# Two attentions of a transformer block's first stage in one sequence of 32 rounds, with other dense products between

## The chip, the cores and the metric

One core of a Trainium2 chip. The metric is the device time of one execution in microseconds. The engines are TensorE (PE), VectorE (DVE), ScalarE (ACT), GpSimd (POOL) and SyncE (SP, which issues the loads); each works through a queue of its own in order, and they wait for one another by semaphores.

## The reference

Float32, 512 tokens of width 1024, a two-block model; only the first stage of the first block is touched. It is two causal attentions over the same normed input, whose outputs are projected together and added to the residual:

```python
a = attn_map(q1, k1) - lam * attn_map(q2, k2)          # differential: 8 heads, halves of 32, values of 64, ALiBi
o = einsum(a, v); o = o * rsqrt(mean(o * o) + eps) * gain
...
sc = einsum(q, k) * 96 ** -0.5                          # latent: 8 heads of 64 + 32 rope dims, values of 64
o = einsum(softmax(where(mask, sc, NEG_INF)), v)        # queries from rank 256, keys and values from rank 128
...
x = x + concat(diff, norm(latent)) @ w_out              # 1024 x 1024
```

The next stage is a cross attention to 256 memory tokens. Its keys and values depend only on the normed memory, and the kernel computes them in the first stage.

## The kernel before, in words

Every dense product is made exact enough by splitting both operands into a high and a low part (`split`, lines 407 and 408, or 410 and 411 with a gain) and adding three products (`mm3`, lines 400 to 402). Activations lie transposed, 128 features by 512 tokens in a tile; a weight block of 128 x 1024 is loaded in 512 KB (line 375) and split, the high part on ScalarE, the low part on VectorE (or GpSimd, where `self.lo_eng` says so). Eight PSUM banks are shared out: two (`pmm`) take all dense products, the column sums of a statistics chain (`stp`, line 438), their broadcast (`stb`, line 451) and the turned rope keys (`psr`, line 1849), in turn; the rest belongs to the attention.

A statistics chain (`stats`) is: squares and their sum on ScalarE, VectorE and GpSimd, column sums on TensorE (438), scaling on VectorE (418), a power on GpSimd (419), the broadcast on TensorE (451) and a copy on VectorE (454).

`mix` (lines 1720 to 2130) is the first stage, 0 to about 320 us. It norms the input, computes the first pair of query and key blocks and half of the values, and goes through 16 rounds of differential attention, four pairs of heads by four blocks of queries: `scores` (products at 1898, minimum 1903, exponentials 1910, combination 1917), `turn` (transposes 1926, copied out at 1929), `values` (1937), and at the end of a pair `normed` (1943 to 1951) and `mixed` (1958). Between the steps of a round `fill(n)` issues dense work from a list of jobs, whose order is the string `MSEQ`, `FILL` = 8 units of three products a round: rope table (r), pairs of query and key blocks (p), values (v), latent queries (c), latent keys (k0) and rope keys (k1), the norms of the latent ranks (n), the memory's norm (m0), keys (m1) and values (m2). `issue_after` holds the dense products of a job behind the scores issued last.

```python
for s_ in steps + [None, None]:
    ...
    now = scores(*s_) if s_ else None
    fill(2)
...
fill(1000)
```

`fill(1000)` issues what is left of the jobs. Then the PSUM banks of the differential attention are given back (one for values, one for transposes, four for scores), and the latent attention takes two for scores, two for transposes, two for values. For each pair of heads: `heads` (two products, gains on VectorE, 2068 and 2071; the key tile, of two in turn, has its rope half copied from `psr` at 1853), scores (2095), minimum (2097), exponentials (2099), division, transposes (2144, copied at 2146), values (2107), the copy of the output (2111) and its split. Last the output projection, eight blocks of columns: `first(c)` multiplies the differential half, the second loop the latent half, whose norm needs a chain over all of the latent output (`stats(oa, ...)`). Two of the `first` blocks stand ahead of that chain.

## Time and profile before

| | us |
|---|---|
| median of 3 runs (lowest to highest) | 2051.84 (2051.07 to 2056.49) |
| the profiled execution: its time | 2053.69 |
| its span in the profile | 2051.9 |
| TensorE busy in the span | 1984.0 |
| VectorE, ScalarE, GpSimd busy | 1024.5, 735.6, 347.7 |
| the first stage | 0 to about 320 |

Products on TensorE are pipelined: a row's duration overlaps the next one's start, so what a product costs is read from the distance of two starts. A plain float32 matrix instruction (scores, transposes, values, statistics) leaves two records in the counts, one product of the three of a dense one a single record. "Busy" does not mean full speed: the granted clock says which of two levels, 2.4 GHz (1.00) or 1.2 GHz (0.50), a stretch ran at. A wait is put down to the instruction that ended it.

### The profile page before, as it was taken

What the parts mean: (1) busy time and instruction counts of PE and PEld (TensorE: products, weight loads), DVE (VectorE), ACT (ScalarE), POOL (GpSimd) and SP (SyncE); (2) the same over time, 40 slices, a digit from 0 to 9 for tenths busy, and PEclk for the clock granted to TensorE, in tenths of its full rate; (3) what the DMA queues carried; (4) which work ended last, traced back from release to release, by engine and by line L of the source; (5) the groups of instructions that cost most, each with busy time, mean ns of one, the idle gap of its engine ahead of it and who ended that gap; (6) DMA issues with size and microseconds to landing.
All of it is one profiled execution on the core that took longest, in us unless ns stands there. A gap on an engine that the chain in (4) does not pass through costs nothing.

```text
span 2051.9 us, 26341 instructions
## 1 busy us (share of the span) xinstructions
PE 1984.0 (97%) x10094; PEld 1521.2 (74%) x10094; DVE 1024.5 (50%) x2067; ACT 735.6 (36%) x1445; POOL 347.7 (17%) x328
## 2 busy tenths in 40 slices
PE   8999999899999999999998999999999999999997
PEld 6768678775555558778877888888876688888886
DVE  7674746632222246788865543343436654434334
ACT  5554644521111133344453332232325642223231
POOL 3012241300000002355411110011111021101111
PEclk9988999999999999999999999999999999999999
DMA  5213114269888852211113222322221033233322
GB/s 191 62 63 108 42 52 159 70 211 391 294 306 331 322 187 64 65 42 53 52 52 102 82 86 85 117 93 81 94 92 42 11 104 102 78 106 105 99 78 70
DMA packets 75458, 243.44 MB, mean 119 GB/s; under 512 B 8825, under 2 KB 11969, under 8 KB 75329
## 3 DMA queue, kind: packets, MB, share of 16 engines
q1 hardware_dynamic: 73520, 240.34, 34.9%
q8 instruction: 81, 1.33, 0.3%
q10 hardware_dynamic: 1664, 1.34, 0.2%
q14 instruction: 49, 0.39, 0.1%
q0 software_dynamic: 144, 0.04, 0.0%
HBM read 235.36 MB, written 6.29 MB: 118 GB/s over the span
## 4 chain that ended last, share of the span: by engine, by line
PE 72%; DVE 3%; DMA 1%; ACT 1%; POOL 1%; issue 0%; DVEq 0%; ACTq 0%
PE mmp L400 16%; PE mmp L401 16%; PE mmp L402 16%; PE pgu L1549 6%; PE psx L1615 3%; PE py L1549 3%; PE pgt L1565 3%; PE sc L1328 1%; DMA raw<-in_w_swa_dram 1%; PE po L749 1%; DVE lo L408 1%; PE tp L962 1%; PE po L1354 1%; PE pt L1340 0%; DVE cv L950 0%; PE sc L729 0%
## 5 line engine op out<-in xcount | busy, mean ns | idle before, releaser
L400 PE MATMUL mmp<-xh,hi 128*128 128x512 f32 (+1 forms) x1328 | 522.2, 393 | 0.8 <-ACT xh L407 0.7
L401 PE MATMUL mmp<-xl,hi 128*128 128x512 f32 (+1 forms) x1328 | 516.9, 389 | 1.0 <-DVE xl L411 1.0
L402 PE MATMUL mmp<-xh,lo 128*128 128x512 f32 (+1 forms) x1328 | 516.7, 389 | 0.0
L407 ACT ACTIVATE hi<-raw 128x1024 fp32r<-128x1024 f32 (+2 forms) x256 | 252.4, 987 | 646.5 <-PE mmp L401 573.7
L408 DVE TENSOR_TENSOR lo<-raw,hi 128x1024 fp32r<-128x1024 f32 (+1 forms) x242 | 280.7, 1161 | 141.5 <-ACT hi L407 138.6
L400 PEld LDWEIGHTS mmp<-xh,hi 128*128 128x128 f32 x1328 | 252.6, 190 | 57.4 <-issue 5.7
L401 PEld LDWEIGHTS mmp<-xl,hi 128*128 128x128 f32 x1328 | 252.6, 190 | 49.9 <-DVE xl L411 1.4
L402 PEld LDWEIGHTS mmp<-xh,lo 128*128 128x128 f32 x1328 | 252.2, 190 | 50.0 <-issue 0.7
L808 POOL TENSOR_TENSOR g<-g,rbc 128x512 f32<-128x512 f32 x44 | 75.1, 1707 | 508.9 <-ACT g L807 508.9
L400 PE MATMUL mmp<-ahi,hi 128*128 128x512 f32 (+1 forms) x374 | 141.9, 380 | 0.0
L401 PE MATMUL mmp<-alo,hi 128*128 128x512 f32 (+1 forms) x374 | 141.9, 380 | 0.0
L402 PE MATMUL mmp<-ahi,lo 128*128 128x512 f32 (+1 forms) x374 | 141.9, 379 | 0.0
L434 POOL TENSOR_TENSOR sqt<-sqt 128x512 f32<-128x512 f32 (+1 forms) x50 | 70.4, 1408 | 252.3 <-ACT sqt L430 236.0
L810 DVE TENSOR_TENSOR a<-mmp,g 128x512 f32<-128x512 f32 x44 | 30.4, 691 | 144.8 <-PE mmp L402 144.8
L806 DVE TENSOR_TENSOR g<-mmp,rbc 128x512 f32<-128x512 f32 x44 | 30.4, 691 | 112.8 <-PE mmp L402 112.7
L400 PEld LDWEIGHTS mmp<-ahi,hi 128*128 128x128 f32 x374 | 70.4, 188 | 14.1
L401 PEld LDWEIGHTS mmp<-alo,hi 128*128 128x128 f32 x374 | 70.4, 188 | 14.0
L402 PEld LDWEIGHTS mmp<-ahi,lo 128*128 128x128 f32 x374 | 70.4, 188 | 14.0
L1565 PEld LDWEIGHTS pgt<-G,tok 128*128 128x128 f32 x512 | 61.6, 188 | 10.9 <-issue 8.9
L1616 DVE TENSOR_TENSOR x<-psx,x 128x512 f32<-128x512 f32 x64 | 43.4, 688 | 47.5 <-PE psx L1615 46.6
L1565 PE MATMUL pgt<-G,tok 128*128 128x256 f32 x512 | 64.6, 282 | 1.0 <-ACT xl L1567 1.0
L1549 PE MATMUL py<-raw,act 128*64 128x512 f32 x256 | 63.9, 599 | 0.2
(519 smaller groups left out, 3001.2 us busy)
## 6 DMA issues: line engine op xcount, KB each, us to landing
raw<-in_w_egu_dram SPq DMA_DIRECT2D x128, 512.0 KB, 7.5
raw<-in_w_gu_dram SPq DMA_DIRECT2D x88, 512.0 KB, 3.5
raw<-in_w_ed_dram SPq DMA_DIRECT2D x64, 512.0 KB, 7.8
raw<-in_w_out_dram SPq DMA_DIRECT2D x24, 512.0 KB, 3.6
raw<-in_w_gdn_dram SPq DMA_DIRECT2D x24, 512.0 KB, 3.6
raw<-in_w_dn_dram SPq DMA_DIRECT2D x32, 384.0 KB, 3.0
raw<-in_w_dn_dram SPq DMA_DIRECT2D x32, 320.0 KB, 2.8
raw<-in_w_qk_dram SPq DMA_DIRECT2D x12, 512.0 KB, 4.3
```

The costliest lines, as they stand in the source:

```text
L400: mm(ps, a[0], b[0], start=first, stop=False)
L401: mm(ps, a[0], b[1], start=False, stop=False)
L402: mm(ps, a[1], b[0], start=False, stop=last)
L407: nc.scalar.activation(hi, src, AF.Copy)
L408: (eng or nc.vector).tensor_tensor(lo, src, hi.bitcast(F32), OP.subtract)
L434: (nc.vector if i == len(chunks) - 1 else nc.gpsimd).tensor_tensor(acc, acc, s, OP.add)
L806: nc.vector.tensor_tensor(g, pg, bc, OP.mult)
L808: nc.gpsimd.tensor_tensor(g, g, bc, OP.mult)
L1549: nc.tensor.matmul(ps[hb], a[:, hb], w[b][:, o:o + 512], start=first, stop=last)
L1565: nc.tensor.matmul(pgt[:, 256 * j:256 * j + 256], toks[k][:, t, cs], G[:, t], start=k + t == 0, stop=k + t == 4)
L1615: nc.tensor.matmul(psx, ys[k][:, a, c * P:(c + 1) * P], ss[a], start=a + k == 0, stop=a + k == 2)
L1616: nc.vector.tensor_tensor(self.x[c], psx, self.x[c], OP.add)
```

## The change

Both attentions become one list of 32 steps, 16 of each, with the same filling between. The list of jobs grows: the memory's norm (m0) comes right behind the rope table, its key blocks (a0 to a3) and value blocks (b0, b1) stand among the query and key blocks, which are now single jobs (x, y), the loads of the latent up-projections (u0, u1), the eight heads (h0 to h7) and the first half of the output projection (f0 to f7, in 256 KB loads) come behind k1. The latent rounds are filled by 2.75 units instead of 8. They keep the banks of the differential rounds: four for scores, one for transposes, one for values. Four key tiles take the rope half from `psr` instead of two. The low parts of weights go to GpSimd from the first latent round on. The second half of the projection has its weights in loads of 256 KB, and four of its blocks take the score banks, ahead of the chain over the latent output. Tiles of scores in SBUF go from nine to seven.

```diff
-MSEQ="r0 p1 v1 p2 c0 c1 p3 k0 k1 n0 m0 m1 m2"
-FILL=8
+MSEQ="r0 m0 x1 a0 y1 a1 b0 a2 a3 b1 x2 y2 v1 c0 x3 y3 c1 k0 n0 u0 u1 k1 h0 h1 h2 h3 f0 f1 h4 h5 f2 f3 h6 h7 f4 f5 f6 f7"
+FILL=(8,2.75)
-SB3=9
+SB3=7
...
-                for k in range(2):
+                for k in range(4):
                     kms.append(M(f"km{k}"))
                     nc.scalar.activation(kms[k][64:], psr[64:], AF.Copy)
+            def g_heads(h):
+                mq, rkv, bkv, ck = lat
+                wu, wq = wuv[:2]
+                ps = self.pmm.tile([P, T], F32, name="mmp", tag="mm")
+                for c in range(2):
+                    gated(ps, wq(c, h * P, (h + 1) * P), cqs[c], c == 0, c == 1)
+                    yield 1
+                qm = F("qm")
+                V.tensor_tensor(qm, ps, mq, OP.mult)
+                ps = self.pmm.tile([P, T], F32, name="mmp", tag="mm")
+                gated(ps, wu(0, h * P, (h + 1) * P), ck, True, True)
+                km = kms[h % 4]
+                V.tensor_tensor(km[:64], ps[:64], bkv[:64], OP.mult)
+                hqk[h] = qm, km
...
+            def g_first(c, w):
+                ps = self.pmm.tile([P, T], F32, name="mmp", tag="mm")
+                for k in range(4):
+                    gated(ps, w(k, 0, P), mix[k], k == 0, k == 3)
+                    if k < 3:
+                        yield 1
+                V.tensor_tensor(self.x[c], ps, self.x[c], OP.add)
+            def w_second(c, eng):
+                raw, hi, lo = self.piece("raw", F32), self.piece("hi", F32R), self.piece("lo", F32R)
+                for k in range(2):
+                    self.last_load = nc.sync.dma_start(raw[:, 512 * k:512 * k + 512], d["w_out"][c + k][:, 512:1024]).ins
+                self.split(hi, lo, raw, eng=eng)
...
+            owed = [0]
             def fill(n):
-                while n > 0:
+                owed[0] += n
+                while owed[0] > 0:
...
+            def lat_scores(c, i):
...
+                sc = [ps_s.tile([P, T], F32, name="sc", tag="sc")[:, :n] for a in range(2)]
+                for a in range(2):
+                    qm, km = hqk[2 * (c - 4) + a]
+                    z = nc.tensor.matmul(sc[a], qm[:, i * P:n], km[:, :n], start=True, stop=True)
+                anchor.append(z.ins)
...
+            def lat_values(c, i, pT):
+                if i == 0:
+                    pos_[c] = ps_o.tile([P, T], F32, name="po", tag="po")
...
-            steps = [(c, i) for c in range(4) for i in range(4)]
-            last, done = None, []
-            for s_ in steps + [None, None]:
+            fill(8)
+            steps = [(c, i) for c in range(8) for i in range(4)]
+            last, done, oa, mix2 = None, [], [], []
+            for s_ in steps + [None]:
...
+                lat_ = int(not s_ or s_[0] > 3)
                 if last:
                     c, i, es = last
                     pT = turn(es, i + 1) if i < 2 else turn(es[:1], i + 1)
-                now = scores(*s_) if s_ else None
-                fill(2)
+                if s_:
+                    if s_ == (4, 0):
+                        self.lo_eng = nc.gpsimd
+                    x = s_[0]
+                    while not (all(t is not None for t in pairs[x]) if x < 4 else 2 * x - 7 in hqk):
+                        fill(0.5)
+                    now = (lat_scores if s_[0] > 3 else scores)(*s_)
+                fill(FILL[lat_] / 4)
...
                     if i > 1:
                         pT += turn(es[1:], i + 1)
-                        fill(2)
-                    values(c, i, 1, pT[1])
+                        fill(FILL[lat_] / 4)
...
+                            oa.append(qp.tile([P, T], F32, name="oa", tag="qk"))
+                            nc.scalar.activation(oa[-1], pos_[c], AF.Copy)
+                            self.split(mix2[0][:, c - 4], mix2[1][:, c - 4], oa[-1], self.sm("mla_out_g", c - 4, c - 3))
+                if s_ == (4, 0):
+                    run(g_vm())
                 if s_:
-                    fill(FILL - (4 if last and last[1] > 1 else 2))
+                    fill(FILL[lat_] * (0.5 if last and last[1] > 1 else 0.75))
                 last = now
             fill(1000)
...
+            w2 = sum((w_second(c, V if c % 4 else nc.gpsimd) for c in range(0, 8, 2)), [])
             _, bc = self.stats(oa, 512, B)
             for c in range(8):
-                ps = self.blk(lambda k, a, b: ws[c](k + 4, a, b), 0, [(mixh[:, k], mixl[:, k]) for k in range(4)])
+                ps = self.blk(w2[c], 0, [(mix2[0][:, k], mix2[1][:, k]) for k in range(4)],
+                              bank=ps_s.tile([P, T], F32, name="sc", tag="sc") if c < 4 else None)
```

How it moves the instructions, at three places. A row is a line of the kernel, an operation, and what it writes from what it reads; x4 counts instructions.

First, TensorE where the values' products of the start end (`hi,xh`, 128x256) and the first block of the jobs begins (`xh,hi`, 128x512). Before:

```order
L401 MATMUL mmp<-lo,xh 128x256
L402 MATMUL mmp<-hi,xl 128x256
L400 MATMUL mmp<-xh,hi 128x512
L401 MATMUL mmp<-xl,hi 128x512
```

Changed:

```order
L401 MATMUL mmp<-lo,xh 128x256
L402 MATMUL mmp<-hi,xl 128x256
L438 MATMUL stp<-ones,sqt 128x1 x2
L1961 MATMUL sc<-qk 128x256 x4
L1961 MATMUL sc<-qk 128x384
L451 MATMUL stb<-cst_all,rt 128x128 x2
L400 MATMUL mmp<-xh,hi 128x512
```

The memory's column sums (438) and their broadcast (451), and scores of a later round (1961), now stand ahead of the first dense product of the jobs.

Second, TensorE at the end of the jobs of the differential rounds. Before, from the last product of k1 on:

```order
L402 MATMUL mmp<-xh,lo 128x512
L1898 MATMUL sc<-qk 128x128 x4
L1958 MATMUL pt<-cst_all,on 128x128 x4
L1937 MATMUL po<-vd_315,pT 128x64 x2
L1898 MATMUL sc<-qk 128x256
L1849 MATMUL psr<-kp,cst_mix 128x512
L438 MATMUL stp<-ones,sqt 128x1 x4
L1898 MATMUL sc<-qk 128x256 x2
L1926 MATMUL pt<-cst_all,s 128x128 x4
L1898 MATMUL sc<-qk 128x256
L451 MATMUL stb<-cst_all,rt 128x128 x4
L438 MATMUL stp<-ones,sqt 128x1 x4
```

Changed, from transposes behind k0's last product to the first of k1:

```order
L1989 MATMUL pt<-cst_all,s 128x128 x4
L451 MATMUL stb<-cst_all,rt 128x128 x4
L438 MATMUL stp<-ones,sqt 128x1 x4
L2000 MATMUL po<-vd_315,pT 128x64
L2000 MATMUL po<-vd_316,pT 128x64
L2000 MATMUL po<-vd_317,pT 128x64
L2000 MATMUL po<-vd_318,pT 128x64
L1989 MATMUL pt<-cst_all,s 128x128 x2
L1961 MATMUL sc<-qk 128x512 x3
L451 MATMUL stb<-cst_all,rt 128x128 x4
L400 MATMUL mmp<-xh,hi 128x512
```

The dense products of k1 now follow the latent norms' two chains; the memory's is gone from here. A little later in the changed order, with buffer numbers, the turned rope keys (`psr`) and the first two heads; a head's query products are 1978 and 2001, its key product 1996:

```order
L1853 MATMUL psr_1937<-kp_1934,cst_mix_220 128x512
L1989 MATMUL pt_1947<-cst_all_113,s_1808 128x128 x3
L400 MATMUL mmp_1978<-cqs_1866,hi_1885 128x512
L401 MATMUL mmp_1978<-cqs_1866,hi_1885 128x512
L402 MATMUL mmp_1978<-cqs_1866,lo_1886 128x512
L400 MATMUL mmp_1978<-cqs_1869,hi_1889 128x512
L401 MATMUL mmp_1978<-cqs_1869,hi_1889 128x512
L402 MATMUL mmp_1978<-cqs_1869,lo_1890 128x512
L400 MATMUL mmp_1996<-cks_1872,hi_1877 128x512
L401 MATMUL mmp_1996<-cks_1872,hi_1877 128x512
L402 MATMUL mmp_1996<-cks_1872,lo_1878 128x512
L400 MATMUL mmp_2001<-cqs_1866,hi_1885 128x512
```

and ScalarE there, changed:

```order
L1992 ACTIVATE pT<-pt 128x512
L1973 ACTIVATE s,smd<-s,mnd 128x512 x4
L407 ACTIVATE xh<-raw 128x512
L1857 ACTIVATE km_1939<-psr 64x512
L1857 ACTIVATE km_1941<-psr 64x512
L1857 ACTIVATE km_1943<-psr 64x512
L1857 ACTIVATE km_1945<-psr 64x512
L1992 ACTIVATE pT<-pt 128x384 x2
```

The dense banks are two, so 1996 takes the bank of `psr`, which four copies on ScalarE read, behind four exponentials (1973).

Third, TensorE in the latent rounds. Before, in the third to fourth query block of the last pair (2095 scores, 2107 values, 2144 transposes):

```order
L2095 MATMUL sc<-km_1443,qm 128x384
L2107 MATMUL po<-pT,vm_2049 64x128
L2144 MATMUL pt<-cst_all,s 128x128
L2095 MATMUL sc<-km_1445,qm 128x384
L2107 MATMUL po<-pT,vm_2049 64x128
L2107 MATMUL po<-pT,vm_2055 64x128 x2
L2107 MATMUL po<-pT,vm_2061 64x128 x2
L2107 MATMUL po<-pT,vm_2067 64x128 x2
L2144 MATMUL pt<-cst_all,s 128x128
L2095 MATMUL sc<-km_1443,qm 128x512
L2107 MATMUL po<-pT,vm_2049 64x128
L2144 MATMUL pt<-cst_all,s 128x128 x2
```

Changed, among the last of f's products (2115 scores, 2136 values, 1989 transposes):

```order
L2136 MATMUL po<-pT,vm_2089 64x128 x2
L2136 MATMUL po<-pT,vm_2095 64x128 x2
L1989 MATMUL pt<-cst_all,s 128x128 x4
L2115 MATMUL sc<-km_1945,qm 128x128
L400 MATMUL mmp<-xh 128x512
L401 MATMUL mmp<-xl,xh 128x512
L402 MATMUL mmp<-xh,xl 128x512
L400 MATMUL mmp<-xh 128x512
L1989 MATMUL pt<-cst_all,s 128x128 x4
L2136 MATMUL po<-pT,vm_2083 64x128
L401 MATMUL mmp<-xl,xh 128x512
L402 MATMUL mmp<-xh,xl 128x512
```

Short groups follow each other before; now products of the output projection stand between them, and the scores are those of a later round.

## Rows read from the trace of the kernel before

**Rows 1.** Of the page: TensorE's busy time, share and instructions, and the row of the clock granted to TensorE in 40 equal slices of the span (51 us each; 9 is 90% or more).

```profile
PE 1984.0 (97%) x10094; PEld 1521.2 (74%) x10094; DVE 1024.5 (50%) x2067; ACT 735.6 (36%) x1445; POOL 347.7 (17%) x328
...
PEclk9988999999999999999999999999999999999999
```

**Rows 2.** Busy time by stage, TensorE alone: from and to, length, TensorE's busy time and records, granted clock, share of the DMA engines, GB/s.

```profile
37.50:131.50 94.00, 92.64 (x552) 1.00 0.24 73
...
203.40:269.60 66.20, 65.21 (x378) 1.00 0.11 33
```

**Rows 3.** The same view in shorter windows, for the clock.

```profile
131.50:136.30 4.80, 1.58 (x17) 0.98 0.00 0
136.30:162.80 26.50, 26.46 (x87) 0.50 0.17 60
162.80:167.00 4.20, 4.20 (x23) 0.52 0.01 4
...
250.00:268.60 18.60, 18.13 (x122) 1.00 0.10 33
...
279.50:282.90 3.40, 3.40 (x13) 0.50 0.22 83
```

**Rows 4.** Timeline of TensorE in a dense stretch: start, duration, line, operation, tiles, shapes, records; a product's duration overlaps the next one's start.

```profile
290.41 0.39 PE L400 MATMUL mmp<-xh,hi 128*128 128x512 f32 x1
290.63 0.39 PE L401 MATMUL mmp<-xl,hi 128*128 128x512 f32 x1
```

**Rows 5.** Timeline of TensorE at the end of the differential attention; in brackets, idle time before a row and what ended it. sc are scores, pt a transpose, stp the column sums of a statistics chain and stb its broadcast.

```profile
131.55 0.50 PE L1898 MATMUL sc<-qk 32*128 32x128 f32 x8
133.06 0.63 PE L1958 MATMUL pt<-cst_all,on 128*128 128x128 f32 x4 [1.00 <-DVE rrd L1947]
...
136.34 1.22 PE L1898 MATMUL sc<-qk 32*128 32x256 f32 x2 [2.26 <-DVE mnd L1903]
...
139.35 1.71 PE L438 MATMUL stp<-ones,sqt 128*128 128x1 f32 x8
...
144.37 2.08 PE L451 MATMUL stb<-cst_all,rt 128*128 128x128 f32 x8
146.23 1.71 PE L438 MATMUL stp<-ones,sqt 128*128 128x1 f32 x8
...
153.56 2.08 PE L451 MATMUL stb<-cst_all,rt 128*128 128x128 f32 x8
```

**Rows 6.** Timelines of VectorE and of TensorE where the first dense product follows the values' products.

```profile
37.42 1.23 DVE L408 TENSOR_TENSOR lo<-raw,hi 128x1024 fp32r<-128x1024 f32 x1
...
37.52 0.40 PE L400 MATMUL mmp<-xh,hi 128*128 128x512 f32 x1
```

**Rows 7.** Groups of instructions, different shapes kept apart, of ScalarE (100 to 270) and GpSimd (0 to 300): line, tiles, shapes, count, busy time in all, mean of one in ns, idle time before and releaser; between them, of line 411 on VectorE, the shortest, median and longest in ns and the first and last start.

```profile
L1910 ACT ACTIVATE s<-s,mnd 128x512 f32<-128x512 f32 x11 | 7.8, 711 | 5.9 <-DVE mnd L1906 5.9
...
L1929 ACT ACTIVATE pT<-pt 128x512 f32<-128x512 f32 x9 | 5.3, 591 | 12.6 <-PE pt L1926 12.6
...
L1853 ACT ACTIVATE km<-psr 64x512 f32<-64x512 f32 x2 | 1.1, 586 | 2.5 <-PE psr L1849 2.5
...
L411 DVE SCALAR_TENSOR_TENSOR xl<-raw,smt,xh x8: 476/477/479, 134.3 to 139.6; 128x256 fp32r<-128x256 f32 x8
...
L408 POOL TENSOR_TENSOR lo<-raw,hi 128x1024 fp32r<-128x1024 f32 x10 | 23.8, 2392 | 36.5 <-ACT hi L407 36.5
...
L419 POOL TENSOR_TENSOR rt<-rp,mhalf 128x2 f32<-128x2 f32 x1 | 0.7, 708 | 6.2 <-DVE rp L418 6.2
```

**Rows 8.** Busy time of TensorE in the latent part, in this order of the tiles mmp (dense products), sc (scores), pt (transposes) and po (values); columns as in rows 2.

```profile
203.40:269.60 66.20, 19.57 (x70) 1.00 0.11 33
...
203.40:269.60 66.20, 22.48 (x64) 1.00 0.11 33
...
203.40:269.60 66.20, 15.73 (x84) 1.00 0.11 33
...
203.40:269.60 66.20, 18.61 (x160) 1.00 0.11 33
```

**Rows 9.** Timeline of TensorE in the latent part: transposes among dense products, then among other short groups.

```profile
209.11 0.60 PE L1958 MATMUL pt<-cst_all,on 128*128 128x128 f32 x4
209.46 0.48 PE L400 MATMUL mmp<-cks,hi 128*128 128x512 f32 x1
...
254.72 0.66 PE L2144 MATMUL pt<-cst_all,s 128*128 128x128 f32 x4
255.22 0.60 PE L2095 MATMUL sc<-km,qm 128*128 128x256 f32 x2
...
259.05 1.09 PE L2107 MATMUL po<-pT,vm 128*64 128x128 f32 x14
260.07 0.33 PE L2144 MATMUL pt<-cst_all,s 128*128 128x128 f32 x1
```

**Rows 10.** Timeline of TensorE at the end of the latent part.

```profile
268.56 1.09 PE L2107 MATMUL po<-pT,vm 128*64 128x128 f32 x14 [0.38 <-ACT pT L2146]
...
278.93 1.58 PE L451 MATMUL stb<-cst_all,rt 128*128 128x128 f32 x8 [2.83 <-POOL rt L419]
```

**Rows 11.** Waits of TensorE from 0 to 320: line, releaser, us in total, times, longest.

```profile
PE stb L451 <- POOL rt L419: 2.8, 1, 2.8
...
PE po L2107 <- ACT pT L2146: 0.4, 1, 0.4
```

More of the change, by code (lines that the diff above doesn't have):

```diff
@@ L1833, in mix @@
             vd = [Vt(f"vd{t}") for t in range(4)]
-            mixh, mixl = self.half()
+            mix = []
             cq, kms, cqs, mem = [], [], [], []
@@ L1849, in g_rope_keys, with gated @@
                 nc.tensor.matmul(psr, self.cst("sel"), kp, start=True, stop=True)
-                for k in range(2):
+                for k in range(4):
                     kms.append(M(f"km{k}"))
                     nc.scalar.activation(kms[k][64:], psr[64:], AF.Copy)
+            def gated(ps, a, b, first, last):
+                with ExitStack() as sa:
+                    if anchor:
+                        sa.enter_context(tc.issue_after(anchor[-1]))
+                    self.mm3(ps, a, b, first, last)
@@ new lines, in w_second, with w_first @@
+            def w_second(c, eng):
[3 more added lines that the diff above has]
+                self.split(hi, lo, raw, eng=eng)
+                return [lambda j, a, b, o=512 * k: [t[:, o + j * P + a:o + j * P + b] for t in (hi, lo)] for k in range(2)]
+            def w_first(c):
+                if not fw:
+                    fw.append(self.half())
+                raw = self.fetch(d["w_out"][c][:, 0:512], 4)[0][0]
+                h, l = (t[:, c % 4] for t in fw[0])
+                self.split(h, l, raw, eng=self.lo_eng)
+                return lambda k, a, b: [t[:, k * P + a:k * P + b] for t in (h, l)]
@@ L1958, in mixed @@
                     nc.tensor.transpose(pt[:, i * P:(i + 1) * P], on[:, i], I)
-                self.split(mixh[:, c], mixl[:, c], pt, gd)
-            jobs, ckv, cs, lat = [], [], [], []
+                if not mix:
+                    h, l = self.half()
+                    mix.extend((h[:, c], l[:, c]) for c in range(4))
+                self.split(*mix[c], pt, gd)
+            jobs, ckv, cs, lat, wuv, hqk, vm, fw = [], [], [], [], [], {}, [], []
             for w in MSEQ.split():
@@ new lines, in lat_values @@
+            def lat_values(c, i, pT):
+                if i == 0:
+                    pos_[c] = ps_o.tile([P, T], F32, name="po", tag="po")
+                for k in range(i + 1):
+                    for a in range(2):
+                        h = 2 * (c - 4) + a
+                        nc.tensor.matmul(pos_[c][64 * a:64 * a + 64, i * P:(i + 1) * P], vm[k][:, h * 64:(h + 1) * 64],
+                                         pT[a][:, k * P:(k + 1) * P], start=k == 0, stop=k == i)
+            run(g_tok(vd, self.load(d["w_v"], 0, 8), hs, rt, 0))
```

158 lines of the change are left out of this document (64 added, 94 removed).

## The prediction

> **What bounds the kernel now.** I read first the page's line of busy time and its row of granted clock: TensorE is busy 97% of the span, so a change of order can only win what TensorE still loses, and the clock row shows those losses' place, a fall in the third slice and again around the sixth [rows 1]. Then the busy time by stage: in the first stage the long dense part (37.5 to 131.5) and the output projection have nearly no idle time, and the latent part is "busy" throughout [rows 2], so what it loses must be found inside the rows. Then the clock in short windows [rows 3], the spacing of the dense products [rows 4], the products at the end of the differential attention [rows 5], and the latent part by kind [rows 8, 9]. Other engines matter only where TensorE waits for them.
>
> Three places lose time in the kernel before.
>
> The end of the differential attention. The dense jobs are used up at 131.5. Until 136.3 TensorE is busy 1.58 of 4.8 us [rows 3]; it waits 1.00 us for a reciprocal and 2.26 us for a minimum [rows 5]. From then to 162.8 it is busy all the time at a granted clock of 0.50, that is 1.2 instead of 2.4 GHz, with statistics, scores and values of the last rounds, and the first 4.2 us of dense products behind that run at 0.52. At full clock the 26.5 and the 4.2 us would be 13.3 and 2.1 shorter; with the 3.2 idle that is 18.6. The busy stretch is itself a row of some twenty short groups, at 0.1 to 0.2 us of start each (four transposes take 0.50 alone, and 0.35 + 0.09 among dense products [rows 9]): 3 more. **21.5 us lost.**
>
> The latent part. A dense product comes every 0.228 us [rows 4]; four transposes among dense ones hold the next up by 0.35 us and make it 0.09 longer, 0.11 each; fourteen short value products take 1.02, 0.073 each [rows 9]. I give a score product the transposes' 0.11 per 128 columns: its 64 records are 16 of each width, 160 units. So the work is 70 x 0.228 + 160 x 0.11 + 84 x 0.11 + 160 x 0.073 = 16.0 + 17.6 + 9.2 + 11.7 = 54.5 of 66.2 us [rows 8]. **11.7 lost**, with hardly a wait on the list [rows 11]: it goes in the starts of short groups that have nothing dense beside them.
>
> The tail. 0.4 us before the last values, 2.83 for the power on GpSimd ahead of the broadcast [rows 10, 11], and 3.4 us at 0.50 [rows 3]: **4.9 lost.**
>
> **The change, part by part.** The products and the bytes loaded are the same, apart from two more copies on ScalarE; only the order and the buffers differ.
>
> *The memory's norm at the start: +5.* Its eight gain-and-split operations on VectorE take 0.477 each [rows 7], 3.8 in all. Before, VectorE was busy without a gap until it came to a weight split at 37.42, and the first dense product followed the values' at 37.52 [rows 6]. In the changed order TensorE has the norm's sums and broadcast ahead of that product. So the sums' scaling comes at about 37.4 + 3.8, the power takes 0.71 [rows 7], the broadcast about 0.5 (four of them took 2.08 at half clock [rows 5]), and the dense products begin at about 42.5: 5.0 later. Scores of later rounds, moved in there, take back 0.9; the clock after five nearly idle us, as behind 131.5, adds about 1. Lower end +1 (splits that fit in while loads are awaited), upper +10 (another 2.1 at half clock and another wait of 2.8, as in the tail).
>
> *The end of the differential attention: -9.5.* One of three chains of statistics (the memory's) is gone from it, and dense products stand around the two that stay. Between the last product of k0 and the first of k1 the new order has two times sums and broadcast, in which the second sums stand behind the first broadcast. Each link went through TensorE, VectorE, GpSimd and back: from the first sums to the first broadcast 5.0 us, from the second sums to theirs 7.3, at half clock [rows 5]. At full clock I take 5.5 for each, 11 in all, with 4.5 of scores, values and transposes in it: 6.5 lost. Next, the key product of the first head needs the bank that the turned rope keys hold (TensorE's two banks for dense work are used in turn). It is freed by four copies of 0.55 on ScalarE, behind four exponentials of 0.71 [rows 7]: 2.2 + 2.9, less the 1.4 of six dense products and the transposes that stand between: 3.5. Half clock around both: 2. Together 12 in the place of 21.5. Lower end -19 (both covered, no fall of the clock), upper +1 (the chains at 7.3 with 10 us at half clock behind them).
>
> *The latent rounds among head products and half the output projection: -8.* With dense products between, the short groups cost their 0.11 and 0.073 and not the start; 3.7 remain for head products that wait for a bank until VectorE has drained it (some 0.7, as ScalarE's exponentials of this size [rows 7]). Lower end -11.7 (nothing lost), upper +17, the slower rival below.
>
> *The tail: +4.* The last four latent rounds have little dense work left. Through the one transpose bank each turn waits for the copy of the one before: 0.59 [rows 7] and the way there and back, three times 0.8, are 2.4. Then the last part of the output is copied, split and multiplied, three operations of 0.6 to 0.75, 2.0 before TensorE goes on. The broadcast still stands directly behind the sums, so the 2.83 stay, and the 1.7 of clock: 8.9 for 4.9. Lower end 0, upper +8.
>
> *The rest: 0.* More rope tables, lazy halves and the second weight split on GpSimd hide under dense work; GpSimd does little here, and a split that came too late would show as a wait before a dense product of the projection. If that cover is gone it costs up to the 2.4 of such a split [rows 7] each time; I count none. Seven tiles of scores instead of nine bind only where scores run more than three rounds ahead.
>
> Sum: +5 - 9.5 - 8 + 4 = -8.5. The profiled execution took 2053.69 (span 2051.9 plus 1.8 around it), 1.9 over the median of the runs shown; the sum goes into the median: 2051.84 - 8.5 = **2043**.
>
> One rule speaks against the change's choice of banks, and a rival rests on the same mechanism, worked out from rows below. The Trainium skill ("Perfetto Trace Analysis", section Matmul Optimizations) asks that all eight PSUM banks be used, so that instructions can run side by side. The trace before agrees as far as it goes: with two transpose banks in the latent part TensorE waited 0.4 us for a copy, all in all [rows 11].
>
> **The rivals.**
>
> *Much faster (18%): 2030.* The chains, the key bank and the start are covered, because the order given to TensorE lets later rounds' scores and dense products come in between. Then 1 + 6 + 3 + 6 are lost in the four places where I have 5 + 12 + 3.7 + 8.9: 13.6 less. For it: the dense part from 37.5 to 131.5 loses almost nothing with the same kind of interleaving [rows 2]. Against: the two chains are in order and need four engines each.
>
> *No change (14%): 2050.* The chains keep 7.3 each and the start costs 8; -9.5 becomes -6 and +5 becomes +8. For it: VectorE and ScalarE are as loaded as before, and each wait lies at the head of TensorE's queue.
>
> *Slower (14%): 2060, the one transpose bank.* The latent rounds keep the differential part's single bank for transposes and single one for values, where two of each were used. In the eight rounds with three or four key blocks there are two turns. The second must wait until the first is copied out, 0.59, on ScalarE behind the exponentials of the next round, two of 0.71; of this 2.0 and about 0.5 for the way, only the filling between the two turns, 0.7 units or 0.5 us, is sure to be covered. That is 2 us a round, 16 to 17 in all. It decides from 1.9 us a round; from there the time is above 2058. For it: ScalarE takes its queue in order. Against: in the new order three to six dense products and the next scores stand between such turns, and the scores run several rounds ahead, so that the exponentials are done early.
>
> *The clock in the latent rounds (5%): 2053.* If transposes and short products there let the clock fall as it did at 136.3, some 20 us of the last rounds would run at 1.2 GHz and cost 10 more. Against: from 250 to 268.6 the latent part is nothing but transposes, scores and short products, and was granted 1.00 [rows 3]. The Trainium skill ("TensorE: Matmul & The Clock Gate", Part 4: PE-mode transpose) says that transposes do not count for the clock as matrix products do; by that rule this case would be likelier than by the row, which shows no fall with 40 transposes among 122 records.
>
> That the change does not do what it says I give no share: the changed order has the head products and the projection's first half among the latent rounds.
>
> **How the numbers follow.** My forecast has 49%, the rivals 18, 14, 14 and 5. 0.3%, or 6.2 us, is about what a measurement tells from no change: faster means below 2045.7, slower above 2058.0. The forecast's own spread (2036 to 2051) lies about four fifths below 2045.7: 39; with the much faster rival's 18 that is 57% faster. Same: 10 of the forecast, 11 of no change, 4 of the clock: 25%. Slower: 3 of no change's upper ends, 14 of the transpose bank, 1 of the clock: 18%. The range 2024 to 2059 leaves out the far side of the much faster case and the upper half of the slowest.
>
> **What would show it.** Right: in the changed profile no stretch at 0.50 of some 30 us around 130 to 160, but two short ones; the first dense product behind the values at about 42; a wait of sums or broadcast of 2 to 4 us twice between k0's and k1's products; a wait for the copies of the turned keys of 3 to 4 before a head product; the latent rounds at 1.00; 8 to 9 us lost between the last values and the second half of the projection. Wrong: a wait of transposes for ScalarE's copies of some 2 us in many latent rounds (the slower rival); a clock below 0.6 over the latent rounds; or none of the three waits (much faster).

## The result, and the profile after

The changed kernel takes **2081.38 us** (median; 2077.76 to 2088.76), the kernel before in the same comparison 2051.45 (2050.05 to 2056.49): 1.46% slower, ratio 1.0146 (95% interval 1.0112 to 1.018). The profiled execution took 2088.76; its span is 2087.0, 35.1 more than the profiled one of before. That execution is the slowest of its four, 7.4 over their median, so its pieces add up to more than the 29.9 between the medians. Marks on TensorE cut the 35.1 into pieces: the start of the first dense product of the jobs; the last values of the latent part; the broadcast of the next stage's first norm, which ends the first stage; and the first column sums (line 471) and the last state product (line 1161) of the second block's recurrent stage, which the change doesn't touch. The first three rows are times from the start, the others lengths.

| us, profiled executions | before | after |
|---|---|---|
| first dense product of the jobs | 37.5 | 45.7 |
| end of the latent part | 269.4 | 307.5 |
| end of the first stage | 328.8 | 347.9 |
| from there to the recurrent stage | 430.9 | 431.0 |
| the recurrent stage | 311.8 | 325.0 |
| from there to the end of the span | 980.5 | 983.1 |

So 19.1 us are lost in the first stage, 13.2 in code that no line of the diff touches, and 2.6 elsewhere. First the page of after, TensorE's busy time and the granted clock, beside [rows 1]:

```profile
PE 1993.7 (96%) x10094; PEld 1527.1 (73%) x10094; DVE 1042.1 (50%) x2058; ACT 736.3 (35%) x1443; POOL 336.9 (16%) x325
...
PEclk9999989999999998999999999999999999999999
```

The fall in the third and fourth slices is gone, as forecast; there is a new one in the sixth (261 to 313 us) and one in the sixteenth. TensorE does the same work in 9.7 us more busy time and waits 25 us longer. By stage (columns as in [rows 2]; the last row lies in the recurrent stage):

```profile
37.50:45.70 8.20, 5.47 (x46) 1.00 0.58 183
45.70:131.50 85.80, 85.80 (x580) 0.98 0.30 101
...
160.00:181.00 21.00, 21.00 (x110) 0.84 0.08 26
...
250.00:270.00 20.00, 15.69 (x78) 0.74 0.26 83
270.00:307.50 37.50, 34.35 (x205) 1.00 0.00 1
307.50:348.00 40.50, 32.31 (x125) 0.83 0.52 185
...
800.00:840.00 40.00, 38.37 (x170) 0.86 0.19 60
```

Where [rows 3] had 26.5 us at 0.50, there are now 21 at 0.84; but 250 to 270 and the tail have both waits and a low clock. Who ended TensorE's waits from 0 to 348, beside [rows 11]:

```profile
PE sc L2115 <- DVE mnm L2121: 5.3, 5, 3.7
PE stb L451 <- POOL rt L419: 2.5, 1, 2.5
...
PE sc L1961 <- DVE mnd L1966: 2.1, 1, 2.1
PE mmp L400 <- DVE om L2195: 2.1, 1, 2.1
...
PE pt L1989 <- ACT pT L1992: 1.3, 2, 0.7
...
PE mmp L400 <- DVE qm L1874: 0.8, 1, 0.8
```

Against the same list of before, the waits ended by VectorE grew by some 10 us, over several lines, and those ended by ScalarE by some 7 (sums over the whole lists; not all their lines are shown). The timeline of after at the places that the argument needs, all engines, beside [rows 5, 6, 9, 10]:

```profile
32.76 1.23 DVE L408 TENSOR_TENSOR lo<-raw,hi 128x1024 fp32r<-128x1024 f32 x1 [2.10 <-ACT hi L407]
33.90 0.68 DVE L454 COPY rbc<-stp 128x512 f32<-128x512 f32 x1
...
44.40 0.91 PE L1961 MATMUL sc<-qk 32*128 32x384 f32 x2 [2.08 <-DVE mnd L1966]
...
45.70 0.48 PE L400 MATMUL mmp<-xh,hi 128*128 128x512 f32 x1
...
168.80 1.45 PE L438 MATMUL stp<-ones,sqt 128*128 128x1 f32 x8
...
174.37 1.90 PE L451 MATMUL stb<-cst_all,rt 128*128 128x128 f32 x8
176.07 0.98 PE L438 MATMUL stp<-ones,sqt 128*128 128x1 f32 x8
...
179.22 1.16 PE L451 MATMUL stb<-cst_all,rt 128*128 128x128 f32 x8
180.13 0.48 PE L400 MATMUL mmp<-xh,hi 128*128 128x512 f32 x1
...
194.25 2.05 ACT L1857 ACTIVATE km<-psr 64x512 f32<-64x512 f32 x4
195.72 0.50 PE L400 MATMUL mmp<-cks,hi 128*128 128x512 f32 x1 [0.78 <-DVE qm L1874]
...
254.06 4.72 POOL L408 TENSOR_TENSOR lo<-raw,hi 128x1024 fp32r<-128x1024 f32 x2 [6.57 <-PE mmp L401]
254.59 0.66 DVE L1878 TENSOR_TENSOR km<-mmp,rbc 64x512 f32<-64x512 f32 x1
255.17 3.76 DVE L2126 TENSOR_SCALAR s<-s,smm 128x256 f32<-128x256 f32 x2
...
259.46 0.80 PE L2115 MATMUL sc<-km,qm 128*128 128x128 f32 x2 [3.65 <-DVE mnm L2121]
...
309.22 2.07 PE L400 MATMUL sc<-xh,hi 128*128 128x512 f32 x4 [1.44 <-ACT xh L410]
...
317.07 2.08 PE L451 MATMUL stb<-cst_all,rt 128*128 128x128 f32 x8 [2.46 <-POOL rt L419]
...
320.68 6.75 POOL L2196 TENSOR_TENSOR x<-x,om 128x512 f32<-128x512 f32 x5 [3.67 <-DVE om L2195]
324.42 3.56 DVE L411 SCALAR_TENSOR_TENSOR xl<-x,smt,xh 128x512 fp32r<-128x512 f32 x2
333.92 0.47 PE L400 MATMUL mmp<-xh,hi 128*128 128x512 f32 x1 [2.06 <-DVE om L2195]
...
340.29 0.50 PE L401 MATMUL mmp<-xl,hi 128*128 128x512 f32 x1 [0.73 <-DVE xl L411]
```

"Lost" is, as in the prediction, the length of a stretch less its products at the full clock's spacing (dense 0.228, short ones as TensorE streams them). In these numbers the first stage loses, before and after: start 13.0, 19.8; dense part 7.1, 11.1; end of the differential attention 22.9, 12.4; latent rounds 16.7, 24.1; tail 4.4, 15.8. That is 64.1 and 83.2, and the difference is the 19.1. Only this total is measured; a single stage's figure moves by some 2 us with the place where the stage is cut and the price put on short products.

### The profile page after: what moved, and what is told of

Read it like the earlier page. It is cut to its first block, busy times and chain, and to the rows that moved or that the text cites. A ratio compares the mean times of both kernels' runs of the same rounds, so it can differ in the third digit from the quotient of the medians.

```text
span 2087.0 us, 26325 instructions
## 1 busy us (share of the span) xinstructions
PE 1993.7 (96%) x10094; PEld 1527.1 (73%) x10094; DVE 1042.1 (50%) x2058; ACT 736.3 (35%) x1443; POOL 336.9 (16%) x325
## 4 chain that ended last, share of the span: by engine, by line
PE 70%; DVE 3%; DMA 1%; ACT 1%; POOL 1%; issue 0%; DVEq 0%; ACTq 0%; POOLq 0%
PE mmp L400 15%; PE mmp L401 15%; PE mmp L402 15%; PE pgu L1549 6%; PE psx L1615 3%; PE py L1549 3%; PE pgt L1565 3%; PE sc L1328 1%; DMA raw<-in_w_swa_dram 1%; PE po L749 1%; DVE cv L950 1%; PE tp L962 1%; DVE lo L408 1%; PE po L1354 1%; ACT hi L407 1%
## 5 line engine op out<-in xcount | busy, mean ns | idle before, releaser
L400 PE MATMUL mmp<-xh,hi 128*128 128x512 f32 (+1 forms) x1280 | 506.2, 396 | 6.4 <-DVE om L2195 2.1
L401 PE MATMUL mmp<-xl,hi 128*128 128x512 f32 (+1 forms) x1280 | 500.5, 391 | 2.3 <-DVE xl L411 2.3
L402 PE MATMUL mmp<-xh,lo 128*128 128x512 f32 (+1 forms) x1280 | 499.8, 390 | 0.0
L407 ACT ACTIVATE hi<-raw 128x1024 fp32r<-128x1024 f32 (+2 forms) x252 | 247.9, 986 | 658.2 <-PE mmp L401 583.3
L408 DVE TENSOR_TENSOR lo<-raw,hi 128x1024 fp32r<-128x1024 f32 (+1 forms) x248 | 289.1, 1167 | 147.1 <-ACT hi L407 145.5
L400 PEld LDWEIGHTS mmp<-xh,hi 128*128 128x128 f32 x1280 | 244.9, 191 | 61.8 <-issue 8.3
L401 PEld LDWEIGHTS mmp<-xl,hi 128*128 128x128 f32 x1280 | 245.0, 191 | 51.2 <-DVE xl L411 3.5
L402 PEld LDWEIGHTS mmp<-xh,lo 128*128 128x128 f32 x1280 | 244.6, 191 | 49.5 <-issue 0.9
L1616 DVE TENSOR_TENSOR x<-psx,x 128x512 f32<-128x512 f32 x64 | 43.4, 688 | 47.4 <-PE psx L1615 46.5
L1549 PE MATMUL pgu<-raw,xh 128*64 128x512 f32 x256 | 61.4, 611 | 2.9 <-PEq L1645 2.9
```

The lines of the kernel that those rows point to most:

```text
L400: mm(ps, a[0], b[0], start=first, stop=False)
L401: mm(ps, a[0], b[1], start=False, stop=False)
L402: mm(ps, a[1], b[0], start=False, stop=last)
L407: nc.scalar.activation(hi, src, AF.Copy)
L408: (eng or nc.vector).tensor_tensor(lo, src, hi.bitcast(F32), OP.subtract)
L1549: nc.tensor.matmul(ps[hb], a[:, hb], w[b][:, o:o + 512], start=first, stop=last)
```

## The experiments

**Is it the order of the recurrent stage?** A scheduler sets each engine's order over the whole program, so the change can reorder code that it doesn't touch. Two transposes that nobody reads, in the changed kernel ahead of the latent statistics, give TensorE and ScalarE the order that they have there before (e1_order); the same two in the kernel before give a third order (e2_border); eleven in the kernel before give the changed kernel's order on TensorE and ScalarE (e12_before_in_afters_order).

```diff
             # e1, e2: range(2); e12: range(11)
+            dmy = ps_t.tile([P, T], F32, name="pt", tag="pt")
+            for _ in range(2):
+                nc.tensor.transpose(dmy[:, :P], oa[-1][:, :P], I)
             _, bc = self.stats(oa, 512, B)
```

> The changed kernel with two more transposes (about 0.2 us) of a finished tile ahead of the latent output's statistics. They change nothing else in the first stage, but the instructions of the second block's recurrent stage, whose code the change does not touch, then stand on TensorE in the order of the kernel before. Theory 'order': 13 us of the 30 lost come from the other order of that stage: the stage (first gate sums to last state product) takes 325.0 us in the changed kernel and would take about 312 here, as before (311.8); the first stage stays as long as changed (348 to the next norm's broadcast); the whole is about 2069. Rival 'after-effect': the stage is slower because of what the first stage leaves behind (clock, loads); then it stays at 325 and the whole at 2081.

> The kernel before with two more transposes (about 0.2 us) at the same place; its recurrent stage then stands in a third order. Theory 'order': the first stage stays at 328.8 to the next norm's broadcast, within 1 us; the recurrent stage is no longer 311.8 but something else, likely 315 to 325, and the whole 2055 to 2066. Rival 'after-effect': nothing changes, 2051 to 2052.

> The kernel before with eleven transposes of a finished tile that nobody reads, ahead of the statistics of its latent half (11 by about 0.11 us, 1.2 us in all); nothing else is edited. The order in which the instructions of the second block's recurrent stage come out is then the changed kernel's on TensorE and on ScalarE (on VectorE and GpSimd it differs from both kernels in places). Theory 'order': the first stage ends at 328 to 331 us as before, and the recurrent stage, 311.8 us in the kernel before, takes 318 to 325 as in the changed kernel and the run with its splits on VectorE; the whole 2059 to 2068. Rival 'first stage': the recurrent stage was longer in the changed kernel for what went ahead of it (the clock, the engines' state), and here takes 308 to 312; the whole 2051 to 2055.

| | end of first stage | recurrent stage | median us | ratio to before |
|---|---|---|---|---|
| e1_order | 346.2 | 310.5 | 2066.50 | 1.0073 (1.0056 to 1.0089) |
| e2_border | 326.9 | 309.7 | 2049.21 | 0.9992 (0.9982 to 1.0001) |
| e12_before_in_afters_order | 329.4 | 324.0 | 2060.21 | 1.0035 (1.0023 to 1.0046) |

It is the order. With the old order the changed kernel's recurrent stage takes 310.5; with the new one the old kernel's takes 324.0, behind a first stage that ends where it did. (e2's third order cost nothing, 309.7, where 315 to 325 was expected.) Over the fourteen kernels of this study TensorE's order in this stage is the changed kernel's in three (325.0, 318.5 and 324.0) and one of five others in eleven (307.9 to 311.8). First a stretch of 40 us at the same place of the stage, TensorE, one row from each run: before, e12, and e3_split_dve (below), which also has the changed kernel's order; after's own row stands above (800 to 840).

```profile
784.00:824.00 40.00, 40.00 (x200) 0.99 0.23 67
...
784.00:824.00 40.00, 38.36 (x176) 0.90 0.18 54
...
794.00:834.00 40.00, 38.15 (x191) 1.00 0.23 67
```

Then the whole stage, one row from each run: before, after, e12 and e3.

```profile
759.70:1071.40 311.70, 298.84 (x1687) 0.97 0.19 57
...
778.90:1103.90 325.00, 307.85 (x1702) 0.95 0.18 56
...
760.30:1084.30 324.00, 306.54 (x1702) 0.96 0.18 56
...
772.90:1091.40 318.50, 300.58 (x1703) 0.98 0.19 57
```

In the 40 us after, e12 and e3 have 170 to 191 records in place of 200: all three wait, and in after and e12 the clock falls as well, in e3 not. Over the whole stage the three are idle for 17.2 to 17.9 us where before is for 12.9. So 4 to 5 us of waits belong to the order; the rest of the 13.2 is busy time, 9.0 more than before in after, 7.7 in e12 and 1.7 in e3, and goes with the granted clock (0.95, 0.96, 0.98). One place can be followed by the rows. Timelines of TensorE, before, after and e12 (the gates' sums, 916, and what is made from VectorE's copy of them, 918):

```profile
801.57 0.38 PE L916 MATMUL gc<-gg,cst_gdn 128*128 128x24 f32 x2
801.79 0.48 PE L402 MATMUL mmp<-xh,lo 128*128 128x512 f32 x1
...
804.17 0.30 PE L918 MATMUL gc<-gc,cst_gdn 128*128 128x24 f32 x2
```

```profile
823.15 0.38 PE L916 MATMUL gc<-gg,cst_gdn 128*128 128x24 f32 x2
824.78 0.62 PE L918 MATMUL gc<-gc,cst_gdn 128*128 128x24 f32 x2 [1.25 <-DVE gc L917]
```

```profile
804.48 0.38 PE L916 MATMUL gc<-gg,cst_gdn 128*128 128x24 f32 x2
806.10 0.62 PE L918 MATMUL gc<-gc,cst_gdn 128*128 128x24 f32 x2 [1.25 <-DVE gc L917]
```

Before, ten dense products stand between 916 and 918; in the other order none does, and TensorE waits, to the hundredth alike in both kernels that have it. The other waits are not followed here. In medians the order is worth 14.9 one way (e1 against after, with 1.7 of it in the first stage) and 7.4 the other (e12, with 1.2 of its own transposes).

**GpSimd's weight splits beside VectorE (e3_split_dve).** The splits of the projection's second half all on VectorE; the recurrent stage keeps after's order.

```diff
-            w2 = sum((w_second(c, V if c % 4 else nc.gpsimd) for c in range(0, 8, 2)), [])
+            w2 = sum((w_second(c, V) for c in range(0, 8, 2)), [])
```

> The changed kernel with the low parts of the second half's output weights split on VectorE alone (before: two of four on GpSimd, at 254.1 to 258.8). The recurrent stage keeps the changed kernel's order on all engines. Theory 'two engines in each other's way': the two divisions of VectorE that took 3.76 instead of about 1.05 beside the GpSimd splits go back, the 3.65 us wait of the scores for the minimum goes with them, and the clock's fall behind it: last latent value 5 to 9 us earlier (307.5 to about 300), the whole 5 to 9 less, 2073 to 2076. Rival 'banks' (the scores' banks and the one transpose bank set the wait): the wait stays, and two more splits of 1.2 on VectorE make it 0 to 2 longer, 2081 to 2083.

Measured: latent part to 301.0 (after 307.5), first stage to 341.4 (347.9), median 2076.22, 5.2 less than after (four runs each, whose ranges overlap). The timeline of e3 in the same rounds, VectorE and then TensorE:

```profile
258.50 0.60 DVE L2126 TENSOR_SCALAR s<-s,smm 128x256 f32<-128x256 f32 x2
```

```profile
256.36 0.50 PE L400 MATMUL mmp<-xh 128*128 128x512 f32 x1 [1.14 <-DVE qm L1874]
...
258.55 0.39 PE L2115 MATMUL sc<-km,qm 128*128 128x128 f32 x2
```

The two divisions (2126) take 0.60 there; beside GpSimd's two splits they took 3.76, and the last ended at 258.93, right behind the second split (258.78). The minimum behind them came late, TensorE waited 3.65 for it, and ran at 1.2 GHz from 259.5 to 268. In e3 250 to 270 was granted 1.00. The Trainium skill ("SBUF — State Buffer", section "SBUF: two separate sides") says that the port pair which VectorE and GpSimd share is locked for a whole instruction and the other engine blocks. The trace agrees, and also in what it lets through: `km<-mmp,rbc` (254.59), which reads PSUM, took its usual 0.66 beside the same split.

**The tail (e4_tail).** Four of the first-half blocks no longer stand ahead of the latent statistics but between the second-half blocks.

```diff
-MSEQ="... h6 h7 f4 f5 f6 f7"
+MSEQ="... h6 h7"
...
+                if c < 4:
+                    run(g_first(c + 4, w_first(c + 4)))
```

> The changed kernel with the first half of only four of the eight output blocks among the latent rounds; the other four stand between the blocks of the second half, behind the statistics, as in the kernel before. Theory 'tail': between the last latent value and the next norm's broadcast TensorE lost about 18 us (40.4 less 100 dense products of 0.2275), against 4.6 before, because the additions, splits and squares of the last blocks come in a bunch on VectorE and GpSimd and the next stage's norm waits for them; with dense products between, 10 of these come back, and the next norm's broadcast comes at about 338 instead of 348. Rival 'cover moved': the latent rounds have less dense work then and lose as much as the tail wins: 348 stays. The recurrent stage stands in an order of its own here, so the whole is 2060 to 2080 and is read by stages.

Measured: first stage to 339.2, 8.7 less than after; median 2064.47, 16.9 less, in which the recurrent stage, in another order, has its share (309.2). The waits for `om` (2.06 at 333.92) and for the last `xl` are gone from the list. That is theory 'tail' (338 expected). In after, four score banks finish at once: four `om` on VectorE, five additions on GpSimd (6.75), and beside these two `xl` in 3.56, where one takes 0.75 in the latent rounds.

**The start (e5_mem_later).** The memory's norm behind the second query and key blocks.

```diff
-MSEQ="r0 m0 x1 a0 y1 a1 b0 ...
+MSEQ="r0 x1 y1 m0 a0 a1 b0 ...
```

> The changed kernel with the memory's norm and first keys behind the pair of query and key blocks x1 and y1, not ahead of them. Theory 'start': the first dense product behind the values comes at 38 to 39 instead of 45.7, TensorE loses 13 instead of 19.8 us up to there, and the next norm's broadcast comes at 340 to 342 instead of 347.9. Rival 'moved stall': the memory's chain then stops the first of its keys' products as long, and the broadcast stays at 347 to 348. The recurrent stage is in an order of its own; the whole is 2060 to 2075 by its stage.

Measured: first dense product at 42.3 (after 45.7, before 37.5), first stage to 344.0, 3.9 less; median 2068.69 (recurrent stage 309.2, in another order). Both expectations missed: 3.4 of the 8.2 us of delay at the start go with the norm's place. The rest stays, because four of the memory's gain splits (line 411, at 31.85) still stand ahead of the input norm's broadcast copy (33.45) on VectorE, and wait 3.32 us, by way of ScalarE, for the load of the memory.

**All three undone (e7_three_undone), and GpSimd kept from weights altogether (e8_no_pool_split).** e7 is e3, e4 and e5 together; e8 also has `self.lo_eng = None` for the latent rounds.

> The changed kernel with three places undone together: the memory later (as in e5), the second half's splits on VectorE (as in e3), four of the eight first-half blocks behind the statistics (as in e4). If the three are separate: the next norm's broadcast at 348 - 7 - 6.5 - 8.7, about 326, and the whole about 2047 with a recurrent stage of 309, 4 below the kernel before. Rival 'shared': they all free the same VectorE time, and the broadcast comes at 332 or later, the whole over 2053.

> As e7, and also the first half's weights split on VectorE: no weight split on GpSimd in the latent rounds. Theory 'two engines in each other's way': 1.3 us pieces on GpSimd cost VectorE little, so within 2 us of e7. Rival 'VectorE is full': the eight splits of 0.6 us on VectorE make head products and scores wait, 3 to 6 us slower than e7.

Measured: first stage to 332.6 and 329.7 (before 328.8), median 2060.46 (ratio 1.0041, 1.0028 to 1.0054) and 2055.78 (1.0015, 1.0004 to 1.0026). The three gave 6.5, 8.7 and 3.9 alone, 19.1 in sum, and 15.3 together; e8 adds 2.9. So these undo 18.2 of the 19.1. e7 came out as the rival 'shared' said. In e8 both expectations missed: it is 4.7 faster than e7 in medians, so GpSimd's shorter splits (most 1.27 us, of 512 columns) had a price too; the longest division is 1.06 us in e7 and 0.77 in e8. What the sequence of 32 rounds then has over the old one is nothing: the 10.5 won at the end of the differential attention are paid elsewhere, as in e8 from 50 to 70, behind the memory's norm, at 0.83 of the clock.

**The good half alone (e6_norms_early), and the banks of the two chains (e9, e10, e11).** e6 is the kernel before with another string only, which takes the latent norms out of the end of the differential attention. e9 is e6 with the sums and broadcasts of the latent norms in a score bank; e10 and e11 are the changed kernel and e8 with the same; `Scores()` stands for the pool of the scores' banks.

```diff
-MSEQ="r0 p1 v1 p2 c0 c1 p3 k0 k1 n0 m0 m1 m2"
+MSEQ="r0 p1 v1 p2 c0 c1 k0 n0 p3 k1 m0 m1 m2"
...
             # e9, e10, e11
-                _, bq = self.stats(cq, 256, B)
+                _, bq = self.stats(cq, 256, B, bank=Scores())
-                rkv, bkv = self.stats(ckv, 128, B)
+                rkv, bkv = self.stats(ckv, 128, B, bank=Scores())
```

> The kernel before with only the order of its jobs changed: the last pair's blocks (p3) and the rope keys (k1) come behind the norms of the latent ranks (n0), so that two of the three statistics chains stand beside dense products. Theory 'end of the differential attention': the 22.9 us lost there become 12 to 15, the next norm's broadcast comes at 319 to 322 instead of 328.8, and the whole is 2040 to 2044 if the recurrent stage takes 310 as in three of the four orders seen. Rival 'one chain is enough': the memory's chain alone still drops the clock for some 25 us, and the broadcast comes at 326 to 329, the whole 2048 to 2052.

> As e6 (the kernel before, latent norms ahead of the last pair's blocks), and the sums and broadcasts of the two latent norms in a bank of the scores' four, not in the two dense banks. Theory 'dense banks': in e6 TensorE still lost 12.4 us from 110 to 130, because sums and broadcasts take the two dense banks in turn and so the next dense products must stand behind the whole chain; with them in a score bank dense products stand between sums and broadcast, 8 to 10 of the 12.4 come back, the clock does not fall there, the next norm's broadcast comes at 313 to 315 instead of 322.4, and the whole is 2038 to 2041. Rival 'score banks': the scores then miss the bank, and as much is lost there: 320 to 323, the whole 2046 to 2049.

> The changed kernel with the sums and broadcasts of the two latent norms in a score bank. Theory 'dense banks': of the 12.4 us lost at the end of the differential rounds 7 to 9 come back, the next norm's broadcast comes at 339 to 341 instead of 347.9; with the recurrent stage in another order than the changed kernel's (309 to 312 instead of 325) the whole is 2057 to 2061. Rival 'score banks': the broadcast stays at 346 to 348, the whole 2065 to 2068.

> As e8 (memory later, no weight split on GpSimd, four first-half blocks behind the statistics), and the latent norms' sums and broadcasts in a score bank. If the places are separate, the next norm's broadcast comes at 329.7 less 5 to 7, about 323 to 325, and the whole 5 to 7 below e8: 2049 to 2051, about as the kernel before. If VectorE sets the pace of the rounds, the gain is given back: within 2 us of e8.

Measured: e6 first stage to 322.4, median 2047.71, ratio 0.9975 (0.9965 to 0.9984): one string, no new buffers, and a little faster than both kernels. The first stage fits its theory (319 to 322), the median lies between theory and rival. e9 2046.10, 0.9967 (0.9955 to 0.998), which e6's interval doesn't exclude; its first stage ends at 323.8, near the 320 to 323 of the rival 'score banks' and not at 313 to 315. e10 ended the first stage at 348.1, as after did (347.9), so there too the rival held; what its median, 2071.14, is below after's comes from the recurrent stage in another order (309.1). e11 2056.95, first stage to 332.0, against 329.7 in e8: no gain. TensorE in windows, e6 and then e9:

```profile
110.00:130.00 20.00, 18.67 (x67) 0.57 0.09 27
...
140.00:160.00 20.00, 19.65 (x129) 1.00 0.36 119
```

```profile
110.00:130.00 20.00, 20.00 (x113) 0.91 0.18 53
...
140.00:160.00 20.00, 17.42 (x69) 0.61 0.24 79
```

The chains still lower the clock where they stand (e6, 0.57), and with banks of their own the weak stretch moves to the end of the differential rounds (e9, 0.61): short groups without dense work are pushed about, not removed.

## Why the prediction was wrong

| step | forecast | measured |
|---|---|---|
| start | +5 | +6.8 |
| end of the differential attention | -9.5 | -10.5 |
| latent rounds | -8 | +7.4 |
| tail | +4 | +11.4 |
| dense part | 0 | +4.0 |
| the rest of the program | 0 | +13.2 in the recurrent stage, +2.6 elsewhere (profiled) |

The first stage was forecast 8.5 shorter and came out 19.1 longer. The terms that failed most are "The rest: 0" and "The latent rounds: -8".

**"The rest: 0"** failed in two ways. It does not mention the code behind the first stage at all, and e1 and e12 show that its new order is worth some 6 to 15 us in medians. And it priced GpSimd's split at the 2.4 that it takes itself, to "hide under dense work"; the split was not late, it held up VectorE's own operations, and e3 and e8 show some 6.5 and 2.9 us of the first stage for that (5.2 and 4.7 in medians). The trace before had a sign of it that I did not read: of its 32 divisions (line 2101), of a median 0.40 us, these two stand beside three of GpSimd's splits (242.21 to 249.28). VectorE, before:

```profile
245.34 1.73 DVE L2101 TENSOR_SCALAR s<-s,smm 128x256 f32<-128x256 f32 x1
247.65 1.85 DVE L2101 TENSOR_SCALAR s<-s,smm 128x384 f32<-128x384 f32 x1
```

The same blocking, then, where TensorE happened to have other work.

**The latent rounds**, -8: wrong in sign. Of the 15.4 us between forecast and result the splits of e3 are 6.5. For the rest, the forecast charged short groups among dense products their bare price and 3.7 us of waits. Even in e3 the waits there come to 6.5 us, mostly for ScalarE's copies and VectorE's bank drains, where the kernel before had 0.7 ([rows 11] have 0.4 of it): filling of 2.75 units does not cover a round's chain of four engines at every turn. So the stretch loses 17.6 us in e3 and 16.7 before, without the waits 11.1 and 16.0: by these sums, an estimate, the dense products did save some 5 us of starts, and the waits took them back.

**The tail**, +4: the power's wait was about right (2.46), and there were two waits of a turn (0.58 and 0.75) for three of 0.8. What it lacked is that four blocks finishing at once jam VectorE and GpSimd (waits of 2.06, 0.77 and twice 0.73), and that the clock falls three times there where it fell once before; e4 gives 8.7 back.

**The start**, +5: the size nearly right, the reason not. The norm's gain splits ran earlier; what came late was the input norm's broadcast copy (33.90, before 29.31), in VectorE's queue behind a weight split that waited for the load of the memory's key weights, and then a minimum of a later round (2.08 at 44.40). The working followed VectorE's operations, and not which loads and splits the new order puts first on SP, ScalarE and VectorE. Of the dense part's +4.0 some 1.7 are dense products at 1.2 GHz right behind it (46.5 to 49.9).

**The end of the differential attention**, -9.5: the size right (12.4 lost, 12 forecast), its parts by luck. The two chains took 5.6 and 3.2 us where 5.5 was taken for each, and TensorE waited for neither broadcast: it was busy 21.00 of the 21 us from 160 to 181, with scores and values of later rounds between, at 0.84 of the clock. The wait before the first key product was 0.78 and not 3.5. That product does not take the bank of the turned keys, as the order was read: it began at 195.72, while the four copies on ScalarE ran on to 196.30, and waited for VectorE's reading of the query product (`qm`). Some 5 of the 12.4 are the clock's (160 to 181 was granted 0.84, 181 to 200 0.91), where the forecast had 2; the rest is starts of short groups and waits under 0.8 us.

Three readings were wrong, at small cost: [rows 1] show the clock's fall in the third and fourth slices and none around the sixth; the start of a short group is 0.06 us in [rows 9] (0.50 against 0.35 + 0.09), not 0.1 to 0.2, so that the "3 more" of the 21.5 are not borne out by them; and a transpose leaves one record, not two (84 records for the latent part's 84 transposes).

The rivals: one transpose bank was not it, waits of transposes for ScalarE are 1.3 us in all, not 16. Nor was it the clock under transposes: 270 to 307.5, nothing but latent rounds and some dense work, was granted 1.00, and the one fall in the latent rounds stands behind the wait of 3.65 us. Of the signs named for a right forecast only the two short stretches at half clock and the full clock in most latent rounds appeared. The slower side came through two mechanisms of which I had neither.

Still open: why the clock falls in the recurrent stage of after and e12 and not at the same place of e3, which has the same order and the same wait (1.2 for 917). And e7's and e8's medians are some 9 and 4 above before's, though their first stages end only 3.8 and 0.9 later and their profiled spans are 2052.2 and 2049.0 against 2051.9: the traces do not show that time.

## What to carry to other kernels

Where a scheduler orders the whole program, compare the order of untouched stages as well, and before judging an edit run it with a dummy instruction or two that shakes that order: here the shake alone was worth a quarter to a half of the loss (7.4 and 14.9 of 29.9). A second engine's spare time is not free when it shares a path with the engine that the rounds wait for; look in the trace before for the maximum, not the mean, of the victim's operations. And take the part that pays by itself first: one string had a quarter of a per cent, where the sequence as a whole had a loss.

## What the hardware showed

Two VectorE divisions of 128x256 took 3.76 us beside GpSimd's splits and 0.60 without; GpSimd's own split did not get slower (2.36 each beside 2.39 in [rows 7]). TensorE was at 1.2 GHz right behind four of after's longer waits (2.08, 3.65, 1.44 and 2.46 us), where dense products came every 0.43 instead of 0.228 us. It was not behind another of the same length (2.06 at 333.92), which had thirteen us of products without a wait ahead of it. It fell again from 343.6 on, behind three shorter waits (0.77 and twice 0.73) close together.
